# Score tiles of one or two PSUM banks: four narrow ones at a time in a fused transformer block

## The chip, the cores and the metric

The kernel runs on one core of a Trainium2 chip. The metric is the device time of one execution in microseconds (us); lower is better. TensorE is called PE below, its weight loads PEld, VectorE DVE, ScalarE ACT, GpSimd POOL, and SyncE, which issues the DMAs, SP.

## The reference

One block of a transformer on a sequence of 1024 positions, 1024 wide: a gated feed-forward network (2816 wide), a mixer, a second feed-forward network, with norms between. The mixer projects the input, runs two attentions and merges them through gates:

```python
# differential attention: 8 heads, two softmaxes each, causal, blocks of 128 queries
s = jnp.einsum('bqhcd,bkhcd->bhcqk', qb, k) * scale
p = softmax(where(kpos <= qpos, s, NEG_INF))
o = einsum('bhqk,bkhe->bqhe', p[:, :, 0] - lam * p[:, :, 1], v)
# sparse attention: 16 heads in 2 groups, three branches, weighted by gates
o = g[..., 0:1] * o_cmp + g[..., 1:2] * o_slc + g[..., 2:3] * o_win
y = x + (sigmoid(g_a) * (y_da @ w_proj_da) + sigmoid(g_b) * (y_ns @ w_proj_nsa)) @ w_out
```

At this length the selected branch (`o_slc`) takes in all earlier blocks, so it is a causal attention; the window branch (`o_win`) sees the last 512 positions. A block of 128 queries with number i (0 to 7) so needs scores against 128(i+1) keys, and in the window branch against at most 640.

## The kernel before, in words

The program is written as tiles from pools, and its waits and the order of instructions on each engine are set when it is built: a planner simulates the time line, and at each step gives an engine the ready instruction of the highest priority. Priority is the order of the program text, moved by offsets. On the chip each engine then follows that fixed order, and an instruction that isn't ready holds up all behind it on its engine.

Stages, in order: first feed-forward network (`ffn`), mixer (`mix`: `prelim`, `da_phase`, `ns_phase`), merging (`proj`), second feed-forward network. Products in fp32 precision are made of three matmuls of high and low parts (`mm3`, lines 52 to 54).

`da_phase` (differential attention) first runs the last projections of the stage before on the PSUM pool `gm0`, four tiles of 128x512 on the right side of PSUM, and closes it (`cg.close()`). Then it loops over 8 heads h and, in each, over m = 0..3, which is two blocks of queries (i = 2m and 2m+1). For each block and each of the two softmaxes, `scores` writes q·k into a score tile `S` in PSUM (L871, two matmuls, or four if the width is over 512), DVE adds the mask in place and finds the row maximum (L878), ACT writes the exponential into SBUF (`Pt`, L880) and so frees the tile. `da_pv` transposes the probabilities on PE into `tr` (L926), ACT and DVE split them (`th` L89, `tl` L85), and PE multiplies them with the values into `o` (L948 to 950). After the scores of each block, `fill.step` puts in a few matmuls of later projections (`gm`, the filler), ordered behind the last score matmul and at a lower priority; it uses PSUM pool `gm1`, one tile.

`ns_phase` (sparse attention) has the same form. Pairs of heads are taken for half H = 0 (m = 0, 1) and then H = 1 (m = 2, 3); each block has a score tile of the selected branch (`Ps`) and one of the window branch (`Pw`). Its matmuls with values are at L1083 and L1084, the compressed branch goes into `o` at L1049, and `ns_fold` (L1092, L1093) empties `o`.

Widths are 128(i+1), so blocks 0 to 3 (m = 0, 1; H = 0) have score tiles of up to 512 columns and blocks 4 to 7 (m = 2, 3; H = 1) of 640 to 1024, in two pieces. All score tiles come from one pool in each attention (`sp1`, `sp2`): two tiles of 1024 columns, which is two banks of 512 each, whatever the width. In each attention the open PSUM pools are, from the left: the scores (2 x 2 banks), `tr` (2), `o` (1), `gm` (1). In the stage ahead, `tr0` (2 banks) and `sc0` (2) lie on the left and `gm0` (4) on the right; in `proj`, `tot2` (2), then `pj` (4).

Every pool is opened with `reuse_waits="tile"`: where a pool lies on banks of a closed one, each of its tiles waits for the users of earlier tiles on its own banks alone.

Of the kernel before, what the change touches and what calls it, by code (L numbers as in the profile page):

```python
# [7 lines left out]
F32 = mybir.dt.float32  # L8
# [10 lines left out]
P = 128  # L19
T = 1024  # L20
TB = 512
# [22 lines left out]
def open_pool(K, ctx, name, bufs, psum=False, side=None):  # L44
    kw = {"space": PSUM} if psum else {}
    if side:
        kw["side"] = side
    return ctx.enter_context(K.tc.tile_pool(name=name, bufs=bufs, reuse_waits="tile", **kw))
# [29 lines left out]
def drain(units):  # L78
    for u in units:
        for _ in u:  # L80
            pass
# [780 lines left out]
        nc.sync.dma_start(out=K.s_pc[u * 2 + pr][tb], in_=pp.bitcast(F32))  # L862


def scores(K, passes, w, mask, nm, pt, l):
    nc = K.nc
    S = K.sp.tile([P, T], F32, tag="S", name="S")
    pieces = [(0, 0, w)] if w <= TB else [(0, 0, w // 2), (TB, w // 2, w // 2)]
    for o, c, n in pieces:
        for i, (q, k, k0) in enumerate(passes):  # L870
            K.last = nc.tensor.matmul(S[:, o:o + n], lhsT=q, rhs=k[:, k0 + c:k0 + c + n], start=i == 0, stop=i == 1)  # L871
    if w <= TB:
        sv, mv, pv = S[:, 0:w], mask, pt[:, 0:w]
    else:
        sv = S.rearrange("p (b c) -> p b c", b=2)[:, :, 0:w // 2]
        mv = mask.rearrange("p (b c) -> p b c", b=2)
        pv = pt[:, 0:w].rearrange("p (b c) -> p b c", b=2)
    nc.vector.tensor_tensor_reduce(out=sv, in0=sv, in1=mv, scale=-0.125, scalar=BIG, op0=ALU.add, op1=ALU.min,  # L878
                                   accum_out=nm)
    return nc.scalar.activation(out=pv, in_=sv, func=AF.Exp, scale=-1.0, bias=nm, accum_out=l)  # L880
# [81 lines left out]
def da_finish2(K, h, H, ob, sq):  # L962
    nc = K.nc
    tot = K.tr.tile([P, TB], F32, tag="tr", name="tot")
    nc.tensor.matmul(tot, lhsT=K.ones, rhs=sq, start=True, stop=True)
    m = K.op.tile([P, TB], F32, tag="sq", name="m")
    nc.vector.tensor_scalar(out=m, in0=tot, scalar1=1.0 / P, scalar2=EPS, op0=ALU.mult, op1=ALU.add)
    y = K.op.tile([P, TB], F32, tag="yr", name="yr")
    z = K.op.tile([P, TB], F32, tag="zr", name="zr")
    newton_rsqrt(nc, y, z, m, nc.gpsimd)  # L970
    nc.vector.scalar_tensor_tensor(out=ob, in0=ob, scalar=K.hgain[:, h:h + 1], in1=y, op0=ALU.mult, op1=ALU.mult)
    yo = [K.op.tile([P, TB], F32R, tag=t, name="yo") for t in ("yr", "zr")]
    split(nc, yo[0], yo[1], ob)
    for i in range(2):
        nc.sync.dma_start(out=K.s_yda[H][h][:, i], in_=yo[i].bitcast(F32))
# [329 lines left out]
def da_phase(K, cg):  # L1305
    nc = K.nc
    with ExitStack() as ctx:
        K.kp, K.vp, K.qp = open_pool(K, ctx, "dk", B_DK), open_pool(K, ctx, "dv", B_DV), open_pool(K, ctx, "dq", B_DQ)
        K.nk, K.vv = {}, {}
        for n, f in enumerate(da_units(K, 0)[:2] + da_units(K, 1)):  # L1310
            if n == 2:
                early = da_load_parts(K, 0)
            if n >= 2:
                next(early)
            if n == 5:
                q0 = da_queries(K, 0, 0)
            drain([f()])
        cg.close()
        K.low = LOW_DA
        log_exp(K)  # L1320
        K.pp, K.sm, K.tp, K.op = (open_pool(K, ctx, "dp", B_DP), open_pool(K, ctx, "dsm", 6), open_pool(K, ctx, "dt", B_DT),
                                  open_pool(K, ctx, "do", 1))
        K.sp = open_pool(K, ctx, "sp1", 2, True)
        K.tr = open_pool(K, ctx, "tr1", TR_DA, True)
        K.ops = open_pool(K, ctx, "o1", 1, True)
        K.gm = open_pool(K, ctx, "gm1", 3 - TR_DA, True)
        pend = K.fin = None

        def finish(h, m, res):
            if m % 2 == 0:  # L1330
                K.o = K.ops.tile([P, TB], F32, tag="o", name="o")
            if K.fin:
                da_finish2(K, *K.fin)
                K.fin = None
            da_pv(K, h, m, res, K.o)
            if m % 2 == 1:
                K.fin = da_finish(K, h, m // 2, K.o)

        ng = NG_DA // 2
        W = K.A["win"]  # L1340
        units = []
        for p in (2, 3):
            cs = [[C_QDA + 2 * p, C_QDA + 2 * p + 1], [C_KDA + 2 * p, C_KDA + 2 * p + 1], [C_VDA + 2 * p], [C_VDA + 2 * p + 1]]
            units += [(f, [W[c] for c in ws]) for f, ws in zip(da_units(K, p), cs)]
        units += [(f, [W[C_GATE + c]]) for c, f in enumerate(gate_units(K, range(16)))]
        units += [(lambda d=d: pda_unit(K, d), [K.A["wda"][d]]) for d in range(KD)]
        fill = K.filler = Filler(K, units)
        for p in range(4):
            fill.pace(4 * (p + 1) if p < 2 else 8 + ng * (p - 1), PACE_DA)
            for h in (2 * p, 2 * p + 1):  # L1350
                if h:
                    da_load(K, h)
                for m in range(4):
                    qt = q0 if h + m == 0 else da_queries(K, h, m)
                    if h == 4:
                        ns_load_key(K, m)
                    res = da_scores(K, h, m, qt, fill.step)
                    if pend:
                        finish(*pend)
                    pend = (h, m, res)  # L1360
            fill.end()
        finish(*pend)
        da_finish2(K, *K.fin)


def ns_phase(K):
    nc = K.nc
    K.low = LOW_NS
    with ExitStack() as ctx:
        K.wslab = open_pool(K, ctx, "wsl", 1).tile([P, 5 * P], F32, name="wslab")  # L1370
        nc.sync.dma_start(out=K.wslab, in_=K.A["wslab"])
        K.qp, K.kp, K.pcp = open_pool(K, ctx, "nq", 2), open_pool(K, ctx, "nk", 1), open_pool(K, ctx, "npc", B_NPC)
        K.pp, K.sm, K.tp, K.op = (open_pool(K, ctx, "np", B_NP), open_pool(K, ctx, "nsm", 6), open_pool(K, ctx, "nt", B_NT),
                                  open_pool(K, ctx, "no", B_NO))
        K.sp = open_pool(K, ctx, "sp2", 2, True)
        K.tr = open_pool(K, ctx, "tr2", 2, True)
        K.ops = open_pool(K, ctx, "o2", 1, True)
        K.gm = open_pool(K, ctx, "gm2", 1, True)
        fill = K.filler
        fill.pace(8 + 16 + KD, PACE_NS)  # L1380
        ns_load_values(K)
        pend = None

        def finish(hd, m, res, st, g, par):
            if m % 2 == 0:
                K.o = K.ops.tile([P, TB], F32, tag="o", name="o")
            ns_pv(K, hd, m, res, K.o, st[0], g, par)
            if m % 2 == 1:
                ns_fold(K, par, K.o, st[1])
                if par:  # L1390
                    ns_out(K, hd // 2, m // 2, st[1])

        for g in range(2):
            for pr in range(4 * g, 4 * g + 4):
                for H in range(2):
                    pc = K.pcp.tile([P, 2, TB], F32R, tag="pc", name="pc")
                    nc.sync.dma_start(out=pc.bitcast(F32), in_=K.s_pc[pr][H])
                    y = K.op.tile([P, TB], F32, tag="y", name="y")
                    for par in range(2):
                        hd = pr * 2 + par  # L1400
                        qt = []
                        for z in range(2):
                            t = K.qp.tile([P, TB], F32R, tag=f"q{z}", name="qt")
                            nc.sync.dma_start(out=t.bitcast(F32), in_=K.s_qns[hd // 4][z:z + 2, :, hd % 4, :, H * TB:(H + 1) * TB]
                                              .rearrange("h a d t -> (h a) d t"))
                            qt.append(t)
                        for m in (2 * H, 2 * H + 1):
                            res = ns_scores(K, hd, m, qt, g, fill.step)
                            if pend:
                                finish(*pend)  # L1410
                            pend = (hd, m, res, (pc, y), g, par)
        fill.end()
        if pend:
            finish(*pend)


def proj(K, open_x, after):
# [54 lines left out]
def body(tc, A, out):  # L1472
    nc = tc.nc
    K = Ctx()
    K.tc, K.nc, K.A = tc, nc, A
    K.low, K.vv, K.gate, K.fill, K.seen = 0, {}, None, None, {}
    K.h, K.acc, K.R = [None] * 2, [None] * 2, [None] * 2
    with ExitStack() as ctx:
        const = open_pool(K, ctx, "const", 1)
# [172 lines left out]
```

## Time and profile before

| | |
|---|---|
| time, median of 3 runs | 2951.38 us (2950.32 to 2952.54) |
| the profiled execution: time, span | 2957.75 us, 2955.7 us |
| PE busy | 2830.8 us, 96% of the span |
| DVE, ACT, POOL busy | 68%, 46%, 27% |
| granted TensorE clock, mean | 0.986 |

The two attentions lie at about 972 to 2109 us of the span. A row of the time line gives start, duration, engine, line, what it writes and reads, the operands' sizes, how many instructions are merged, and in brackets the idle time of the engine before it with what ended that. A row of waits gives the total, how often, and the longest.

### The profile page before, as it was taken

What the parts mean: (1) busy time and instruction counts of PE and PEld (TensorE: products, weight loads), DVE (VectorE), ACT (ScalarE), POOL (GpSimd) and SP (SyncE); (2) the same over time, 40 slices, a digit from 0 to 9 for tenths busy, and PEclk for the clock granted to TensorE, in tenths of its full rate; (3) what the DMA queues carried; (4) which work ended last, traced back from release to release, by engine and by line L of the source; (5) the groups of instructions that cost most, each with busy time, mean ns of one, the idle gap of its engine ahead of it and who ended that gap; (6) DMA issues with size and microseconds to landing.
All of it is one profiled execution on the core that took longest, in us unless ns stands there. A gap on an engine that the chain in (4) does not pass through costs nothing. (4 is left out here: it accounts for less than half of the span.)

```text
span 2955.7 us, 40158 instructions
## 1 busy us (share of the span) xinstructions
PE 2830.8 (96%) x14276; PEld 2129.2 (72%) x14276; DVE 2002.1 (68%) x3347; ACT 1366.1 (46%) x2347; POOL 788.7 (27%) x701
## 2 busy tenths in 40 slices
PE   8999999999999899989899999999999999999998
PEld 6644447888888678778788888888778854444886
DVE  7866856666687467667677777776343877675666
ACT  7543424442332245445466666666332653342443
POOL 3133321000144123322233323332242413333001
PEclk9999999999999999999999999999999999999999
DMA  4355548655456544444332234222742246454854
GB/s 161 129 194 180 182 161 287 214 172 170 146 200 240 173 161 168 170 165 164 122 115 79 86 119 155 79 84 76 281 158 100 89 147 230 149 185 158 297 182 146
DMA packets 212711, 478.20 MB, mean 162 GB/s; under 512 B 20896, under 2 KB 39584, under 8 KB 212512
## 3 DMA queue, kind: packets, MB, share of 16 engines
q1 hardware_dynamic: 212512, 475.65, 47.1%
q8 instruction: 112, 1.84, 0.3%
q14 instruction: 87, 0.71, 0.1%
HBM read 313.56 MB, written 162.00 MB: 161 GB/s over the span
## 5 line engine op out<-in xcount | busy, mean ns | idle before, releaser
L405 PEld LDWEIGHTS <-w 128*128 128x128 f16 x3024 | 297.1, 99 | 381.1 <-issue 30.4
L52 PE MATMUL gm<-hi,whi 128*128 128x512 f32 x880 | 351.5, 399 | 4.0 <-ACT whi L89 1.6
L54 PE MATMUL gm<-hi,wlo 128*128 128x512 f32 x880 | 348.3, 397 | 1.1 <-DVE wlo L85 1.1
L53 PE MATMUL gm<-lo,whi 128*128 128x512 f32 x880 | 348.0, 395 | 0.0
L405 PE MATMUL Y<-tf,w 128*128 128x512 f16 x1296 | 296.7, 383 | 19.1 <-DVE u L443 15.6
L871 PE MATMUL S<-kt,qt 128*128 128x320 f32 (+5 forms) x1152 | 274.6, 352 | 37.5 <-ACT Pt L880 12.0
L85 DVE TENSOR_TENSOR tl<-tr,th 128x512 fp32r<-128x512 f32 (+2 forms) x384 | 236.3, 619 | 89.0 <-ACT th L89 85.5
L89 ACT ACTIVATE th<-tr 128x512 fp32r<-128x512 f32 (+2 forms) x384 | 203.7, 542 | 200.4 <-PE tr L926 195.6
L85 DVE TENSOR_TENSOR wlo<-st,whi 128x1024 fp32r<-128x1024 f32 x154 | 197.6, 1300 | 113.5 <-ACT whi L89 112.2
L878 DVE CUSTOM_DVE_ANT_0 S<-S,slab 128x896 f32<-128x896 f32 (+7 forms) x320 | 224.7, 709 | 65.8 <-PE S L871 61.3
L53 PE MATMUL acc<-wlo,whi 128*128 128x512 f32 (+1 forms) x628 | 244.1, 389 | 1.0 <-DVE wlo L85 1.0
L89 ACT ACTIVATE whi<-st 128x1024 fp32r<-128x1024 f32 x154 | 160.7, 1057 | 178.2 <-PE acc L54 111.6
L54 PE MATMUL acc<-whi,wlo 128*128 128x512 f32 (+1 forms) x628 | 242.8, 389 | 0.0
L52 PE MATMUL acc<-whi 128*128 128x512 f32 (+1 forms) x628 | 240.4, 387 | 0.0
L871 PEld LDWEIGHTS S<-kt,qt 128*128 128x128 f32 x1152 | 183.4, 190 | 61.5 <-ACT Pt L880 13.8
L1037 POOL TENSOR_SCALAR Ps<-Ps,l 128x384 f32<-128x384 f32 (+7 forms) x128 | 100.7, 787 | 428.6 <-DVE l L1035 214.4
L405 PE MATMUL X<-h,w 128*128 128x512 f16 x864 | 195.3, 379 | 0.5 <-ACT s L415 0.5
L52 PEld LDWEIGHTS gm<-hi,whi 128*128 128x128 f32 x880 | 168.3, 191 | 37.2 <-ACT whi L89 2.2
L54 PEld LDWEIGHTS gm<-hi,wlo 128*128 128x128 f32 x880 | 167.8, 191 | 37.3 <-DVE wlo L85 1.8
L53 PEld LDWEIGHTS gm<-lo,whi 128*128 128x128 f32 x880 | 168.1, 191 | 30.9
L85 DVE TENSOR_TENSOR wlo<-wst,whi 128x1024 fp32r<-128x1024 f32 x103 | 135.8, 1320 | 45.4 <-ACT whi L89 36.1
L1083 PE MATMUL o<-th,vt 128*128 128x256 f32 (+1 forms) x608 | 165.0, 288 | 1.6 <-ACT th L89 1.5
(320 smaller groups left out, 6128.7 us busy)
## 6 DMA issues: line engine op xcount, KB each, us to landing
wst<-in_win_dram SPq DMA_DIRECT2D x55, 512.0 KB
sw<-w2s SPq DMA_DIRECT2D x44, 512.0 KB
st<-sw SPq DMA_DIRECT2D x88, 256.0 KB
st<-saT SPq DMA_DIRECT2D x88, 256.0 KB
a<-in_f1w_dram SPq DMA_DIRECT2D x36, 512.0 KB
a<-in_f2w_dram SPq DMA_DIRECT2D x36, 512.0 KB
st<-saB SPq DMA_DIRECT2D x66, 256.0 KB
qt<-sq SPq DMA_DIRECT2D x128, 128.0 KB
```

Source lines behind the costliest of these rows:

```text
L52: first = nc.tensor.matmul(out, lhsT=w[0][:, wk], rhs=x[0], start=start, stop=False, skip_group_check=skip)
L53: nc.tensor.matmul(out, lhsT=w[0][:, wk], rhs=x[1], start=False, stop=False, skip_group_check=skip)
L54: nc.tensor.matmul(out, lhsT=w[1][:, wk], rhs=x[0], start=False, stop=stop, skip_group_check=skip)
L85: return nc.vector.tensor_tensor(out=lo, in0=src, in1=hi.bitcast(F32), op=ALU.subtract)
L89: nc.scalar.activation(out=hi, in_=src, func=AF.Copy)
L405: K.mark = nc.tensor.matmul(o, lhsT=w[:, a, m * h + k], rhs=x[k][:, b], start=start and k == 0 and i == 0, stop=k == h - 1 and i == 2, ski ...
L871: K.last = nc.tensor.matmul(S[:, o:o + n], lhsT=q, rhs=k[:, k0 + c:k0 + c + n], start=i == 0, stop=i == 1)
L878: nc.vector.tensor_tensor_reduce(out=sv, in0=sv, in1=mv, scale=-0.125, scalar=BIG, op0=ALU.add, op1=ALU.min, accum_out=nm)
L1037: nc.gpsimd.tensor_scalar(out=p[:, 0:n], in0=p[:, 0:n], scalar1=l[:, c:c + 1], scalar2=1.0, op0=ALU.mult, op1=ALU.mult)
L1083: nc.tensor.matmul(dst, lhsT=v, rhs=hi[:, b * P:(b + n) * P], start=False, stop=False, skip_group_check=True)
```

## The change

`scores` takes its tile from a new function `score_tile`. Up to 512 columns the tile is one bank, from a pool of four such tiles; above, it is two banks, from a pool of two. The pool is opened when the first tile of a width class is asked for, and closed and opened anew where the class changes; it lies on the right side of PSUM. The fixed pools `sp1` and `sp2` go, and each attention ends with a `close_scores`.

```diff
+def score_tile(K, w):
+    n = 1 if w <= TB else 2
+    if K.s_banks != n:
+        close_scores(K)
+        K.sp, K.s_banks = open_pool(K, K.s_ctx, "sp", 4 // n, True, side="right"), n
+    return K.sp.tile([P, n * TB], F32, tag="S", name="S")
+
+
+def close_scores(K):
+    K.s_ctx.close()
+    K.s_ctx, K.s_banks = ExitStack(), 0
+
+
 def scores(K, passes, w, mask, nm, pt, l):
     nc = K.nc
-    S = K.sp.tile([P, T], F32, tag="S", name="S")
+    S = score_tile(K, w)
...
@@ da_phase
-        K.sp = open_pool(K, ctx, "sp1", 2, True)
         K.tr = open_pool(K, ctx, "tr1", TR_DA, True)
...
         da_finish2(K, *K.fin)
+        close_scores(K)
...
@@ ns_phase
-        K.sp = open_pool(K, ctx, "sp2", 2, True)
         K.tr = open_pool(K, ctx, "tr2", 2, True)
...
             finish(*pend)
+        close_scores(K)
...
@@ body
+    K.s_ctx, K.s_banks = ExitStack(), 0
```

The other pools of an attention so move to the left: `tr` to the first two banks, then `o`, then `gm`; the scores take the last four.

## The prediction

> **What bounds the kernel now.** I read the page first, then busy times by stage, then what PE waited for in each stage, then the time line around the longest waits.
>
> ```profile
> span 2955.7 us, 40158 instructions
> PE 2830.8 (96%) x14276; PEld 2129.2 (72%) x14276; DVE 2002.1 (68%) x3347; ACT 1366.1 (46%) x2347; POOL 788.7 (27%) x701
> L871 PE MATMUL S<-kt,qt 128*128 128x320 f32 (+5 forms) x1152 | 274.6, 352 | 37.5 <-ACT Pt L880 12.0
> ```
>
> PE is the bound: 125 us of its span are idle, and 37.5 of them lie ahead of score matmuls. The change moves no arithmetic off PE, so it can win only idle time. By stage (the columns are the stretch, its length, then busy time and count for PE, PEld, DVE, ACT, POOL, the granted clock, the DMA share, GB/s):
>
> ```profile
> 963.00:1040.00 77.00, 63.30 (x273) 51.32 (x273) 37.59 (x71) 20.73 (x38) 11.48 (x11) 0.91 0.50 172
> 1040.00:1455.00 415.00, 390.19 (x2061) 330.82 (x2060) 297.17 (x611) 207.13 (x425) 116.25 (x116) 0.98 0.47 162
> 1455.00:1480.00 25.00, 17.36 (x84) 14.23 (x85) 9.91 (x21) 9.50 (x21) 4.86 (x5) 0.80 0.34 115
> 1480.00:2090.00 610.00, 588.27 (x3752) 523.93 (x3751) 440.87 (x1134) 382.22 (x882) 187.82 (x259) 0.99 0.30 101
> ```
>
> These rows are the start of the differential attention, its body, the passage to the sparse attention, and that one's body. PE is idle 13.7, 24.8, 7.6 and 21.7 us in them. A score tile is freed by the exponential of L880, so a score matmul that waits for a free tile shows as a wait for ACT at L880. The waits of PE, first for the body of the differential attention, then for the sparse one:
>
> ```profile
> PE S L871 <- ACT Pt L880: 10.9, 7, 5.7
> PE o L948 <- ACT th L89: 3.9, 1, 3.9
> ...
> PE S L871 <- ACT Ps L880: 7.1, 14, 1.0
> PE o L1049 <- DVE y L1093: 5.2, 7, 1.1
> PE o L1084 <- DVE tl L85: 4.0, 15, 0.3
> PE S L871 <- ACT Pw L880: 3.3, 8, 0.9
> ```
>
> So waits for a score tile cost PE 10.9 us in the one and 10.4 us in the other. That 21.3 us, 0.7% of the time, is what more tiles could touch at most, and only the part in narrow blocks (up to 512 columns) is touched at all: a wide block has two tiles of two banks before and after.
>
> **The change part by part.** It adds and removes no instruction of the engines; it changes how many narrow tiles are open, which banks the pools have, and through both the order that the planner writes.
>
> *Sparse attention, narrow blocks.* One narrow stretch (H = 0 of a pair of heads) and the wide one behind it, then the time line of its start on PE and ACT:
>
> ```profile
> PE S L871 <- ACT Ps L880: 1.0, 2, 0.8
> PE o L1049 <- DVE y L1093: 0.6, 1, 0.6
> PE o L1084 <- DVE tl L85: 0.6, 2, 0.3
> PE S L871 <- ACT Pw L880: 0.4, 1, 0.4
> ...
> PE S L871 <- ACT Pw L880: 0.2, 1, 0.2
> ```
>
> ```profile
> 1538.96 0.44 PE L871 MATMUL S<-kt,qt 128*128 128x128 f32 x2 [0.22 <-ACT Ps L880]
> 1540.51 0.44 PE L871 MATMUL S<-kt,qt 128*128 128x128 f32 x2 [0.78 <-ACT Ps L880]
> 1544.80 0.39 PE L871 MATMUL S<-kt,qt 128*128 128x256 f32 x1 [0.39 <-ACT Pw L880]
> 1537.70 1.11 ACT L880 ACTIVATE Ps<-S,nm 128x1024 f32<-128x1024 f32 x1 [1.95 <-PE tr L926]
> 1539.99 0.37 ACT L880 ACTIVATE Ps<-S,nm 128x128 f32<-128x128 f32 x1 [0.22 <-DVE nm L878]
> ```
>
> The first narrow tile (1538.96) waited for the last 1024-wide exponential, which ends at 1538.81. After the change it needs a bank of that same wide tile, so its 0.22 us stay. The second (1540.51) waited for the first narrow one's exponential (1539.99 + 0.37); after, it takes the other bank of the wide tile and goes at once: 0.78 won. The third (1544.80) waited for the other wide tile; a bank of the first narrow tile has been free since 1540.36: 0.39 won. That is 1.17 of the 1.39 us. I found this pattern in five of the eight narrow stretches (from 1538, 1615, 1767, 1846 and 1997): 5.9 us. The first stretch (from 1478) has waits of its own, 1.04, 0.86 and 0.17 us, all between narrow tiles: 2.1 us. Together 8.0 us. What is late next is in the same rows: `o` waits for `ns_fold` (0.6) and for `tl` (0.6) in each stretch, and PE comes to them earlier by what it won. I let a quarter go there: −6 us, bounds −8 and −2.
>
> The Trainium skill, "TensorE: Matmul & The Clock Gate", section "HAM oscillation", reports a kernel in which PSUM double-buffering gave no further gain once the order of its loops kept PE fed. Here PE is 96% fed (588.27 of 610), so as a rule it speaks against this change: this term would be near 0 instead of −6, and the sum near no change. No row of before can show which it is; the rows above have PE idle before score tiles all the same, and the sum goes by them.
>
> *Differential attention, narrow blocks.* Of the 10.9 us three waits, 7.3 us, stand before narrow tiles; the matmul's size and count tell narrow from wide (two matmuls, not four):
>
> ```profile
> 1253.54 0.50 PE L871 MATMUL S<-kt,qt 128*128 128x256 f32 x2 [0.33 <-ACT Pt L880]
> 1270.58 1.22 PE L871 MATMUL S<-kt,qt 128*128 128x512 f32 x2 [5.67 <-ACT Pt L880]
> 1411.19 0.44 PE L871 MATMUL S<-kt,qt 128*128 128x128 f32 x2 [1.27 <-ACT Pt L880]
> 1269.37 0.60 ACT L89 ACTIVATE vh<-tr 128x512 fp32r<-128x512 f32 x1 [5.61 <-DMA sv<-vh]
> ```
>
> The long one is not for want of tiles in itself: ACT stood 5.61 us behind a filler's copy that waited for a store to land, and the exponential was queued behind it. With four tiles that score matmul would not have waited, and PE had `o` products and a filler behind it; but an ACT that stands stops the next thing too, and the new order needn't put the copy at that place. I take half: −3.7 us, bounds −7.3 and 0.
>
> *Start of the differential attention.* This is where the banks move. Before, the scores lie on the banks of `tr0` and `sc0`, long free, while the last projections still run on `gm0`. So the planner let the first scores run ahead among them:
>
> ```profile
> 963.00:1036.00 73.00, 7.03 (x32) 5.94 (x32) 0.91 0.51 173
> 972.05 0.45 PE L871 MATMUL S<-kt,qt 128*128 128x128 f32 x1 [4.31 <-issue]
> 977.83 0.66 PE L871 MATMUL S<-kt,qt 128*128 128x128 f32 x2 [4.26 <-DMA kt<-sk]
> 1011.48 0.66 PE L653 MATMUL tr<-ident,vt 128*128 128x128 f32 x4 [2.63 <-DVE vt L650]
> 1021.18 0.66 PE L653 MATMUL tr<-ident,vt 128*128 128x128 f32 x4 [1.05 <-DVE vt L650]
> 993.42 1.23 DVE L85 TENSOR_TENSOR rl<-m,rh 128x1024 fp32r<-128x1024 f32 x1 [12.25 <-DMA sq<-rl]
> ```
>
> The first row is the score matmuls alone: 7.0 us of PE up to 1036. After the change the scores lie on the right, on `gm0`'s own banks, and the first one has to wait until the last projections have emptied them, so these 7.0 us move behind. Against it, the two waits of 4.31 and 4.26 us, in which PE held the projections back for a score operand that had not landed, go. But the next bound there is already in the rows: DVE stood 12.25 us until 993.42 for a store to land, and the projections' results can't be evicted before that; with four banks PE would run about 21 us from 967 (24 matmuls at 0.23 us a tile, four tiles) and stop at 989. So I count the 8.6 us as turned into a wait for eviction, except some 2 us for an earlier restart. Of the 7.0 us, about 2.5 us were in the shadow of the waits at 1011 and 1021 and of the lower clock (0.91 in the first row), and return as idle or fall away. So −2 + 4.5 = +2.5 us. Ends: −8.6 (both waits go and nothing replaces them) and +11 (all 7.0 exposed, and 4 us of the first chain from score to transpose, of the size of the 4.3 us waits above, with no filler to cover it, since the filler is ordered behind the first score).
>
> *End.* `pj` of `proj` lay on banks of `S` and `tr`; after, its four are those of `o`, `gm` and two of `S`.
>
> ```profile
> 2109.30 0.44 PE L52 MATMUL pj<-yl,whi 128*128 128x512 f32 x1
> 2110.12 0.69 DVE L1093 TENSOR_TENSOR y<-o,y 64x512 f32<-64x512 f32 x1 [1.26 <-ACT y L1092]
> ```
>
> If the planner gives the first tile `o`'s bank, it waits for the fold, to 2110.81: 1.5 us. Three other banks are free, so I take +0.3, bounds 0 and +1.5. *Changes of width.* From narrow to wide, a wide tile needs two neighbouring banks, at worst with the last narrow tile in one; before, the second wide tile waited for it anyway. I count nothing, up to +3 over 16 changes of about 0.2 us, the size of the wide waits above. *DMA queue, POOL.* Nothing is moved past them; 0. *New order as such.* The planner's clock isn't the chip's; the 3.9 us wait for `th` shows what one misplacement costs, either way: 0, ±6.
>
> Sum: −6 − 3.7 + 2.5 + 0.3 = −6.9 us. The profiled execution took 2957.75 us (span 2955.7), 6.4 us over the median of 2951.38; the difference is applied to the median: 2944.5 us, −0.23%. Differences within 0.2%, 5.9 us, can't be told from no change here.
>
> **The rivals.**
> (a) *The stalls only change their names.* In the sparse attention the chain from transpose through `th` and `tl` to `o`, and the fold, take over what the tile waits leave; the differential one's long wait comes back elsewhere. For it: DVE is 72% and ACT 63% busy there (440.87 and 382.22 of 610). Against: waits at the fold and `tl` are short (0.3 to 1.1). With −2, 0 and the start's +2.5: 2952 us.
> (b) *Slower through the start.* Scores locked out by `gm0`: +11 there, with −2 and −2 kept of the two gains: 2958 us. It decides from about +10 at the start if the gains hold fully. For it: the row of 7.0 us run ahead. Against: PE's own stalls at 972 and 978 go.
> (c) *Pool by pool.* Reopening makes the first tile of a new width wait for all tiles of the old pool. A tile's chain at 512 columns is about 1.5 us (DVE 0.7, ACT 0.7 by their rows' rates), at some 30 changes, half covered: +22, with the sum 2966 us. Against: the pools are declared to wait tile by tile.
> (d) *The start gains too.* Both 4.3 us waits go without a successor, and the narrow waits go fully: −8 − 7.3 − 2 = 2934 us.
>
> **How the numbers follow.** Chances: forecast 0.40 (its own range 2938 to 2950), (a) 0.22, (b) 0.16, (c) 0.06, (d) 0.16. Faster by over 0.2%: (d) and three quarters of the forecast, 0.46. Same: a quarter of the forecast and (a), 0.32. Slower: (b) and (c), 0.22. The range takes in the forecast, (a), most of (d) and (b): 2932 to 2958.
>
> **What would show it.** Right: waits of narrow `S` for ACT at L880 in the sparse attention down from about 9 us to under 3; no score matmul before the last `gm0` projection; the gaps at 972 and 978 gone, with idle PE around 990 to 1000. Wrong: scores still among the projections; new long waits of PE for `th`, `tl` or the fold; waits at the first tile of each width. The whole would be wrong if the new order moved a DMA-bound wait into or out of the differential attention, which no row of before can tell.

## The result, and the profile after

The changed kernel is slower: 2996.24 us median (2994.45 to 2999.07) against 2951.96 us, a ratio of 1.0149 (95% interval 1.0132 to 1.0167). Its profiled execution took 2994.96 us, span 2992.9 us. From its page (columns as before):

```profile
span 2992.9 us, 40061 instructions
PE 2836.7 (95%) x14276; PEld 2130.5 (71%) x14276; DVE 2004.5 (67%) x3347; ACT 1367.3 (46%) x2347; POOL 794.0 (27%) x701
L884 PE MATMUL S<-kt,qt 128*128 128x320 f32 (+5 forms) x1152 | 260.3, 350 | 23.0 <-ACT Pw L893 6.9
```

The idle time ahead of score matmuls fell from 37.5 to 23.0 us, as intended, and yet PE's idle time rose from 125 to 156 us. (`scores` moved down by 13 lines: L884 was L871, the exponential L893 was L880.) The two attentions as two stages, from 963 to the first sparse score matmul and from there to the first `pj`; first before, then after:

```profile
963.00:1456.00 493.00, 453.53 (x2334) 382.22 (x2333) 335.45 (x683) 228.04 (x463) 128.59 (x128) 0.97 0.48 164
1456.00:2109.00 653.00, 622.51 (x3942) 552.11 (x3942) 458.17 (x1165) 398.68 (x914) 191.81 (x263) 0.99 0.32 108
```

```profile
963.00:1488.00 525.00, 462.70 (x2343) 387.84 (x2341) 336.71 (x681) 229.85 (x463) 134.71 (x129) 0.94 0.45 154
1488.00:2149.00 661.00, 624.28 (x3950) 552.11 (x3950) 461.95 (x1169) 400.12 (x916) 193.56 (x264) 0.99 0.32 108
```

The first stage takes 32 us longer: 22.8 us more idle PE (62.3 against 39.5) and 9.2 us more busy time, at a clock of 0.94 instead of 0.97. Not all of it is lost there. Up to the first score matmul PE has the same order of matmuls in both kernels, and yet this execution is already 3.6 us behind at 963; its first stage so holds 0.8% more matmul columns (909,184 against 902,144), some 3.5 us of the 9.2. The sparse attention takes 8 us longer, 6.2 of them idle.

The start, on PE's time line:

```profile
1005.61 0.80 PE L52 MATMUL gm<-hi,whi 128*128 128x512 f32 x1 [12.49 <-ACT whi L89]
...
1038.47 1.86 PE L884 MATMUL S<-kt,qt 128*128 128x128 f32 x7 [1.41 <-DVE vl L85]
```

The lockout is there: the first score matmul comes at 1038.47 instead of 972, and the two waits of 4.3 us have become one of 12.49 us. PE's waits in the body of the differential attention (1040 to 1456), then in the sparse attention (1520 to 2140):

```profile
PE gm L52 <- DVE vl L85: 12.6, 2, 12.1
PE o L961 <- DMA vt<-sv: 8.0, 3, 3.7
PE S L884 <- DMA qt<-sq: 6.6, 5, 3.9
PE o L962 <- DVE tl L85: 4.6, 4, 2.3
PE gm L52 <- DVE m L626: 4.0, 3, 2.1
PE S L884 <- ACT Pt L893: 2.6, 4, 1.0
```

```profile
PE o L1097 <- DVE tl L85: 11.4, 30, 2.4
PE o L1096 <- ACT th L89: 7.0, 9, 3.1
PE S L884 <- ACT Pw L893: 6.9, 22, 0.6
```

In the first, the wait for a score tile fell from 10.9 to 2.6 us, and five other names took its place. In the second, the waits for `Ps` and the fold are gone (7.1 and 5.2 us before), those for `Pw` rose from 3.3 to 6.9, and `o` waits 18.4 us for `tl` and `th`. The longest stall, followed through SP, ACT and DVE:

```profile
1267.32 0.69 DVE L85 TENSOR_TENSOR yo<-ob,yo 128x512 fp32r<-128x512 f32 x1
...
1275.47 4.76 SPq L988 DMA_DIRECT2D syd<-yo  x1
1281.00 1.09 SPq L988 DMA_DIRECT2D syd<-yo  x1
...
1287.54 0.63 ACT L155 ACTIVATE yr<-m 128x512 f32<-128x512 f32 x1 [10.44 <-DMA syd<-yo]
1290.19 0.60 ACT L89 ACTIVATE vh<-tr 128x512 fp32r<-128x512 f32 x1 [2.02 <-DMA sv<-vh]
1290.83 0.69 DVE L85 TENSOR_TENSOR vl<-tr,vh 128x512 fp32r<-128x512 f32 x1 [12.56 <-ACT vh L89]
...
1291.58 0.79 PE L52 MATMUL gm<-hi,whi 128*128 128x512 f32 x1 [12.08 <-DVE vl L85]
```

`yo`, a head's normalised result, is done at 1268.01; its store waits its turn on SP until 1275.47, and the second half until 1281.00. The next norm (`yr`) shares `yo`'s buffer, so ACT stands 10.4 us; the filler's copy `vh` is behind it on ACT, `vl` behind that on DVE, and PE's next filler needs the bank that `vl` empties. But `vh` then stands 2.02 us more for a store of its own buffer (`sv<-vh`), issued on SP at 1282.18, behind the second half of `yo`. So without the wait of `yr` this stall would have ended hardly earlier; what both waits share is SP's queue.

### The profile page after: what moved, and what is told of

The parts are those of the page before. It is cut to its first block, busy times and chain, and to the rows that moved or that the text cites. A ratio compares the mean times of both kernels' runs of the same rounds, so it can differ in the third digit from the quotient of the medians.

```text
span 2992.9 us, 40061 instructions
## 1 busy us (share of the span) xinstructions
PE 2836.7 (95%) x14276; PEld 2130.5 (71%) x14276; DVE 2004.5 (67%) x3347; ACT 1367.3 (46%) x2347; POOL 794.0 (27%) x701
## 5 line engine op out<-in xcount | busy, mean ns | idle before, releaser
L405 PE MATMUL Y<-tf,w 128*128 128x512 f16 x1296 | 297.1, 384 | 21.8 <-DVE u L443 18.4
L884 PE MATMUL S<-kt,qt 128*128 128x320 f32 (+5 forms) x1152 | 260.3, 350 | 23.0 <-ACT Pw L893 6.9
L884 PEld LDWEIGHTS S<-kt,qt 128*128 128x128 f32 x1152 | 184.2, 192 | 41.5 <-ACT Pw L893 12.2
L1097 PE MATMUL o<-tl,vt 128*128 128x256 f32 (+1 forms) x608 | 158.5, 293 | 13.0 <-DVE tl L85 12.5
```

The costliest lines, as they stand in the source:

```text
L405: K.mark = nc.tensor.matmul(o, lhsT=w[:, a, m * h + k], rhs=x[k][:, b], start=start and k == 0 and i == 0, stop=k == h - 1 and i == 2, ski ...
L1097: nc.tensor.matmul(dst, lhsT=v, rhs=lo[:, b * P:(b + n) * P], start=False, stop=last, skip_group_check=True)
```

## The experiments

**The three parts of the change.** T1: the banks (the lockout) are the loss. T2: the four tiles, through the order that the planner writes. T3: reopening. Also T0: any new order is a new throw.

Banks alone (two tiles of two banks, not reopened):

```diff
-        K.sp = open_pool(K, ctx, "sp1", 2, True)
+        K.sp = open_pool(K, ctx, "sp1", 2, True, side="right")
...
-        K.sp = open_pool(K, ctx, "sp2", 2, True)
+        K.sp = open_pool(K, ctx, "sp2", 2, True, side="right")
```

> Only the banks move: the two score tiles of two banks are opened on the right, so that they lie on gm0's banks, and tr, o and gm come first on the left; two tiles everywhere, nothing reopened. T1 (the lockout at the start, and what follows from the banks): the change's loss is here; no score matmul before the last gm0 projection, first score near 1038 us instead of 972, and the time 15 to 44 us over before (some 2967 to 2996). T2 (four narrow tiles let the planner write an order with more stalls): the start alone costs, about +10 to +15 at the head of DA4, and the time ends at +7 to +15, with the differential attention's later stalls (the 12.1 us at 1291 of after) absent. T0 (any new order re-rolls what the planner and the chip disagree on): anywhere from -5 to +30, with stalls at places that neither before nor after has.

The change without the banks (the scores on the left; `gm`, `o` and `tr` opened on the right, on the banks of before):

```diff
-        K.sp, K.s_banks = open_pool(K, K.s_ctx, "sp", 4 // n, True, side="right"), n
+        K.sp, K.s_banks = open_pool(K, K.s_ctx, "sp", 4 // n, True), n
...
```

> The change with its banks as before: narrow blocks have four tiles, wide ones two, the pool is reopened where the width changes, but the scores stay on the left (free when the first score comes) and tr, o and gm on the banks that they had before. T1: scores run ahead among the last projections again (about 7 us of score matmuls before 1036), and the time is -7 to 0 against before. T2: the start is as before, and still the time is 15 to 30 us over before, with long waits in the body of the differential attention and waits of o for th and tl in the sparse one (18 us together against about 5 in before). T0: between.

Reopening alone; against the kernel just described:

```diff
-        K.sp, K.s_banks = open_pool(K, K.s_ctx, "sp", 4 // n, True), n
-    return K.sp.tile([P, n * TB], F32, tag="S", name="S")
+        K.sp, K.s_banks = open_pool(K, K.s_ctx, "sp", 2, True), n
+    return K.sp.tile([P, T], F32, tag="S", name="S")
```

> Reopening alone: two tiles of two banks for every width, on the left, the pool closed and opened again where the width changes. T1 and T2: within 3 us of before. T3 (reopening is what costs, by waits at the first tile of a new width or by the order that it makes): 15 to 30 us over before, as much as with four narrow tiles.

Two tiles, reopened, on the right (the changed kernel with the edit just shown, the side kept):

> The changed kernel with two tiles of two banks in place of four of one: scores on the right (gm0's banks), reopened at each change of width. With two tiles on the right and no reopening the time was +18.5 us over before; with reopening and two tiles on the left it was -11.5; the change itself +44. If four tiles are what costs: +5 to +20 over before (2957 to 2972). If it is the lockout together with reopening: +35 to +45.

Four narrow tiles on the left in one attention only, the other as before:

```diff
+    if K.s_ctx is None:
+        return K.sp.tile([P, T], F32, tag="S", name="S")
...
```

> Four narrow tiles in the sparse attention alone, on the left with the pool reopened; the differential attention is before's. By the prediction: -6 us (waits of narrow scores for the exponential down from 9 us to under 3, nothing in their place). By T2: +6 us, as after's sparse attention lost 6.2 from its first score to the first pj: the waits for a score tile fall, and o's waits for th and tl rise from about 5 to about 18 us. By T1: as the prediction, -6 to 0.

> Four narrow tiles in the differential attention alone, on the left (no lockout), with the pool reopened; the sparse attention is before's. With four narrow tiles in both (scores on the left) the kernel took 35 us more than before: +28 at the head of the sparse attention and +8 at its start. T2 (four narrow tiles change the order, and the loss is in the differential attention) says +22 to +30, with ACT waiting 20 us or more in all for the store of the head's result before it may write the next norm (yr, zr), as in the run with four tiles in both. T1 (banks alone) says within 5 us of before.

Three narrow tiles in place of four:

```diff
-        K.sp, K.s_banks = open_pool(K, K.s_ctx, "sp", 4 // n, True), n
+        K.sp, K.s_banks = open_pool(K, K.s_ctx, "sp", 3 if n == 1 else 2, True), n
```

> Three narrow tiles of one bank in place of four, else as four on the left (2987) and two on the left, reopened (2941). Theory B: between them, nearer to four, as two exponentials more than two tiles allow are still one too many: ACT's wait for the buffers 15 to 40 us, the time 2955 to 2980. If each order is its own throw: anywhere from 2935 to 2990, with no tie to that wait.

Measured, with before; "first sparse" and "to pj" are the time of the first sparse score matmul and the length from there to the first `pj`, from PE's time line of each trace, and each ratio is against runs of the kernel before that were taken with it. One trace differs from another by some us even where nothing was changed: at 963, ahead of every edit's effect on PE's order, these traces lie 1.6 us ahead of before's to 4.7 us behind it.

| score tiles | side | reopened | first sparse | to pj | median | ratio (95%) |
|---|---|---|---|---|---|---|
| two (before) | left | no | 1456.0 | 653.4 | 2952 | 1 |
| two | right | no | 1474.0 | 653.8 | 2970.69 | 1.0065 (1.0050 to 1.0080) |
| two | left | yes | 1454.9 | 641.4 | 2940.78 | 0.9963 (0.9948 to 0.9977) |
| two | right | yes | 1470.2 | 643.1 | 2959.13 | 1.0015 (1.0003 to 1.0028) |
| three narrow | left | yes | 1477.9 | 658.8 | 2980.36 | 1.0108 (1.0091 to 1.0124) |
| four narrow | left | yes | 1482.7 | 660.7 | 2987.23 | 1.0124 (1.0107 to 1.0141) |
| four narrow (after) | right | yes | 1488.1 | 661.0 | 2996.24 | 1.0149 (1.0132 to 1.0167) |
| four, sparse only | left | there | 1454.6 | 657.3 | 2959.99 | 1.0030 (1.0020 to 1.0039) |
| four, differential only | left | there | 1486.2 | 654.5 | 2981.77 | 1.0100 (1.0085 to 1.0115) |

The rows fit together. Banks alone came out in T1's range (+18.5 us), four tiles on the left a little over T2's (+35, of 15 to 30). The four tiles cost 46 us on the left (2987.23 to 2940.78) and 37 on the right: T2 is the loss, and T1 alone is not, since with no lockout at all the four tiles still end 35 us over before. The banks cost 18 us with two tiles, 9 with four. T3 turned out the other way: reopening by itself gains 11.5 us on either side. It acts in the sparse attention (641.4 against 653.4 and 643.1 against 653.8); the first sparse score comes only 1.1 and 3.8 us earlier. In the sparse attention each kind of tiles has its own length, to a few microseconds: about 654 us with two tiles, 642 reopened, 657 to 661 with four (or three) narrow ones. Compared matmul by matmul, PE has the same order there on both sides with two tiles reopened, and nearly the same in the two kernels with two that are not. T0 alone would not repeat itself so well. The effects of the four tiles in the two attentions add up: 7.8 + 29.3 = 37.1 against 35.0. Three tiles cost nearly as much as four; 2980.36 is at the edge of the 2955 to 2980 that was forecast.

**Why four tiles cost in the sparse attention.** The stage with two tiles, reopened, then with four tiles in it only; PE's matmuls there have the same number of columns in both (1,117,184):

```profile
1454.90:2096.30 641.40, 617.47 (x3944) 546.99 (x3945) 454.12 (x1165) 399.78 (x914) 194.09 (x263) 0.99 0.32 111
```

```profile
1454.60:2111.90 657.30, 624.36 (x3944) 552.27 (x3945) 460.22 (x1166) 399.80 (x914) 193.81 (x263) 0.99 0.32 108
```

Four tiles have 9.0 us more idle PE (32.9 against 23.9) and 6.9 us more busy time. PE's waits with four, then with two (both 1500 to 2090), and on the time line what stands at the start with four:

```profile
PE o L1099 <- DVE tl L85: 8.0, 27, 0.7
PE S L886 <- ACT Pw L895: 6.9, 22, 0.6
PE o L1098 <- ACT th L89: 3.5, 7, 0.6
```

```profile
PE o L1097 <- DVE tl L85: 6.8, 25, 0.5
PE o L1096 <- ACT th L89: 3.4, 6, 0.7
PE S L884 <- ACT Pw L893: 2.2, 8, 0.4
```

```profile
1492.06 0.63 ACT L89 ACTIVATE yo<-ob 128x512 fp32r<-128x512 f32 x1 [4.18 <-DVE ob L986]
1493.12 0.38 PE L1098 MATMUL o<-th,vt 128*128 128x256 f32 x1 [3.12 <-ACT th L89]
...
1497.89 1.16 DVE L85 TENSOR_TENSOR tl<-tr,th 128x384 fp32r<-128x384 f32 x2 [3.81 <-DMA syd<-yo]
1498.50 0.58 PE L1099 MATMUL o<-tl,vt 128*128 128x256 f32 x1 [2.57 <-DVE tl L85]
```

Past the start `o` waits about as long as with two tiles (11.5 against 10.2 us); there it is the score matmuls that wait more, for `Pw`. The rest of the idle time is at the start. With four tiles the scores and the fillers go out nearly in one run from 1476 to 1490; next in PE's order is `o`, and it waits. Its `th` stands on ACT behind the last head's norm of the differential attention (4.18 us), its `tl` on DVE for that head's store (3.81 us). In the kernel before, that run lasts from 1479 to 1497, and `o` follows it without a wait. The longer busy time goes with a lower granted clock around these gaps: 0.86 against 0.93 from 1456 to 1500, 0.94 against 1.00 from 1500 to 1540.

**Why they cost in the differential attention: the buffers behind the score tiles.** An exponential reads a score tile and writes into one of seven buffers (`dp`, 4 KB a partition each), which is freed when DVE has combined the two softmaxes (`Pt`, L927) or PE has transposed the result (L939). ACT's waits for such a buffer from 1040 to 1456, in before (the same figures with two tiles reopened), in after, and with four tiles on the left:

```profile
ACT Pt L880 <- DVE Pt L914: 3.3, 2, 2.6
```

```profile
ACT Pt L893 <- DVE Pt L927: 36.7, 18, 4.3
```

```profile
ACT Pt L893 <- DVE Pt L927: 41.2, 20, 3.1
...
ACT Pt L893 <- PE tr L939: 11.0, 4, 5.1
```

This separates all the kernels with seven buffers: 0.7 to 3.3 us with two tiles, 36 us or more with three or four. ACT works in order, so while it stands for a buffer, the copies behind it (`th`, `vh`, the norms) stand too. That the wait goes with the loss doesn't show yet that it makes it, so I changed the number of buffers both ways. Six, with two tiles:

```diff
-B_DP = 7
+B_DP = 6
```

> Two tiles of two banks, reopened, on the left, with six buffers for the exponentials' results in place of seven. Theory B: the same signature as with four tiles comes back, ACT waiting 20 us or more for DVE's Pt and PE's tr, and +10 to +40 us against 2941. Rival (the buffers don't bind): within 6 us of 2941.

```profile
ACT Pt L893 <- DVE Pt L927: 10.9, 7, 2.7
...
ACT Pt L893 <- PE tr L939: 8.4, 5, 5.0
```

The time was 2966.25 us (1.0050, 1.0035 to 1.0065), 25 us over the same kernel with seven, and the first sparse score at 1472.7 instead of 1454.9: the wait came back with the loss. It isn't alone there: ACT's wait for the fillers' weights rose as well, from 5.5 to 22.1 us. Eight, at the price of a query buffer:

```diff
-B_DQ = 4
+B_DQ = 3
...
-B_DP = 7
+B_DP = 8
```

> Four narrow tiles on the left, with eight buffers for the exponentials' results (dp, seven so far) and three for the queries (dq, four so far; the room for the eighth). In the kernels with four narrow tiles ACT waits 36 to 55 us of the differential attention for such a buffer (for DVE's Pt and for PE's tr, which free it), in those with two 1 to 3 us. Theory B (the limit moved from the score tiles to these buffers, and ACT, in order, stands with the copies of everything else behind it): that wait falls below 20 us and the time comes 15 us or more below four tiles with seven buffers (2987), nearer to its two-tile control. Rival (the stores on SP's queue around 1240 to 1350, or the lost cover of o, set it): the wait may fall, the time stays within 8 us of 2987 by more than the control moves.

> The control: two tiles of two banks, reopened, on the left, with the same eight and three buffers. With two tiles ACT waits 3 us for such a buffer, so an eighth is worth nothing; three query buffers may cost. Theory B: 0 to +12 us against two tiles with seven buffers (2941), all of it by later queries.

This told nothing: 3013.83 us (1.0213, 1.0198 to 1.0228) with four tiles, 2978.12 (1.0094, 1.0079 to 1.0109) with two; both waited for queries, 46.0 and 37.5 us (differential attention, to 1480), where 12 us of loss at most was forecast for the second.

So I took the room from the mask instead, with a control of seven each. Of the mask only the right half is kept, so these kernels mask the first half of a wide block wrongly; every instruction keeps its size:

```diff
-        K.slab = cst.tile([P, T], F32, name="slab")
-        nc.sync.dma_start(out=K.slab, in_=A["slab"])
+        K.slab = cst.tile([P, TB], F32, name="slab")
+        nc.sync.dma_start(out=K.slab, in_=A["slab"][:, TB:T])
...
+def half_mask(K, w):
+    if w <= TB:
+        return K.slab[:, TB - w:TB]
+    return K.slab[:, TB - w // 2:TB].unsqueeze(1).broadcast_to([P, 2, w // 2])
...
```

> Four narrow tiles on the left with eight buffers for the exponentials' results and all four query buffers; the room comes from the mask, of which only the right half is kept, so that wide blocks read that half twice (their mask is wrong in the first half, every instruction keeps its size). Theory B (the buffers of the results are the limit that the two extra tiles run into): ACT's wait for a buffer in the differential attention (54 us with four tiles and seven buffers) falls to under 35 and the time lies 10 to 30 us below the control with seven buffers and the same mask. Rival C (the planner's order with more tiles ahead meets the stores and the lost cover whatever the buffers): within 8 us of that control.

> The control for four tiles: the half mask alone, seven result buffers. All theories: within 5 us of four tiles on the left with the whole mask (2987), as no size of an instruction and no order changes.

> Two tiles of two banks, reopened, on the left, with eight result buffers, four query buffers and the half mask. Theory B: two tiles hardly wait for a buffer (3 us), so within 6 us of the control with seven (some 2941). If an eighth gains 10 us or more here, the buffers bind in both and don't explain the difference.

> The control for two tiles, reopened: the half mask alone, seven result buffers. All theories: within 5 us of the same with the whole mask (2941).

ACT's waits with four tiles and eight buffers, then with seven (1040 to 1456):

```profile
ACT Pt L899 <- DVE Pt L933: 27.1, 13, 3.6
...
ACT yr L155 <- DMA syd<-yo: 22.5, 4, 7.1
...
ACT Pt L899 <- PE tr L945: 3.6, 3, 2.0
...
ACT zr L157 <- DMA syd<-yo: 2.5, 1, 2.5
```

```profile
ACT Pt L899 <- DVE Pt L933: 41.0, 20, 3.1
...
ACT zr L157 <- DMA syd<-yo: 20.6, 3, 12.3
ACT yr L155 <- DMA syd<-yo: 18.8, 4, 11.2
...
ACT Pt L899 <- PE tr L945: 10.8, 4, 5.1
```

Four tiles: 2982.51 us with eight (1.0104, 1.0087 to 1.0121), 2992.11 with seven (1.0131, 1.0114 to 1.0148). Two tiles: 2942.48 (0.9966, 0.9955 to 0.9978) and 2946.06 (0.9979, 0.9970 to 0.9988). The controls lie 4.9 and 5.3 us over the same kernels with the whole mask, though PE's matmuls come in the same order. The wait for buffers fell from 51.8 to 30.7 us (both names), and the eighth buffer is worth 9.6 us to four tiles and 3.6 to two; the theory had asked for 10 at least. Nor is it clean: with four tiles the eighth buffer also changed PE's order in the differential attention, and PE's waits there (1040 to 1480) mostly changed their names: those for a score tile fell from 18.9 to 2.3 us, those for `th` rose from 8.2 to 11.2, for queries from 0.6 to 10.4, for `vl` to 9.2. It is a part, not the whole.

**The norm that waits for a store.** In the rows above ACT also waits 25.0 us (eight buffers) and 39.4 us (seven) for the head's store before it may write `yr` or `zr`. With four tiles on the left PE's longest wait of the differential attention, for a score tile, stands behind one of these, the exponential being next on ACT:

```profile
PE S L884 <- ACT Pt L893: 17.8, 6, 10.0
```

```profile
1342.12 0.63 ACT L157 ACTIVATE zr<-yr 128x512 f32<-128x512 f32 x1 [12.37 <-DMA syd<-yo]
...
1343.25 1.22 PE L884 MATMUL S<-kt,qt 128*128 128x512 f32 x2 [9.96 <-ACT Pt L893]
```

So there the wait for a score tile rose with four tiles, from 10.9 to 17.8 us (first row, 1040 to 1456). I took the store's wait away: the store reads a tile that stays (in the first two kernels the mask, in the last two a cosine table), so that `yo` is free at once and what is stored is not the heads' result.

```diff
-        nc.sync.dma_start(out=K.s_yda[H][h][:, i], in_=yo[i].bitcast(F32))
+        nc.sync.dma_start(out=K.s_yda[H][h][:, i], in_=K.slab[:, 0:TB])
```

> The changed kernel, but the 32 stores of the differential attention's normalised heads take the mask as their source instead of yo: the same DMAs of the same size at the same place, and no buffer of yo is held until its store lands (the values stored are not the heads'). In after, ACT waited 16 us in all (10.4 us the longest) for that store before it could write yr, and PE lost 12.1 us at 1291 behind it. If that wait is the loss of the differential attention's body: that stall is gone and the time is 12 to 22 us below after (2974 to 2984). If the stall is only the name of a new order that is short of DMA: another wait of 6 to 12 us stands in its place and the time is within 6 us of after.

> The same edit in the kernel before, as the control: in before ACT waited for that store 8.9 us in two places before 1500, none of which stopped PE for long. Expected: 0 to -5 us against before. If it gains as much as in the changed kernel (12 us or more), the store's wait is a loss of both kernels and does not explain their difference.

The changed kernel gained 14 us (2981.90; 1.0094, 1.0078 to 1.0111), the kernel before 7.6 (2944.91; 0.9978, 0.9969 to 0.9988), where 5 at most was forecast; so this wait explains some 7 us of their difference. And the stall at 1291 stayed, under another name:

```profile
1289.24 0.60 ACT L89 ACTIVATE vh<-tr 128x512 fp32r<-128x512 f32 x1 [10.03 <-DMA sv<-vh]
```

PE's filler at 1292.13 waited 11.02 us behind it. The store ahead of it on SP is now not ACT's problem; the filler's own store, on the same queue, is. Last, the eighth buffer and the free store together:

> Four narrow tiles on the left, eight result buffers, half mask, and the 32 stores of the normalised heads take their data from a table that stays (the values stored are not the heads'), so that no norm waits for a store. With eight buffers alone four tiles took 2982.5, ACT still waiting 25 us for those stores and 34 us for result buffers. If buffers and stores together are the loss of four tiles: 15 us or more below 2982.5, and within 20 us of its two-tile control. If the new order as such is (waits that only change names): within 10 us of 2982.5, and 30 us or more over the control.

> The control with two tiles, reopened: eight result buffers, half mask, the same stores from the table. With two tiles ACT hardly waited for stores or buffers (under 1 us each), so -8 to +2 us against the same kernel with yo stored (2942.5).

2972.16 us (1.0067, 1.0044 to 1.0089) with four tiles, 2940.44 (0.9958, 0.9945 to 0.9972) with two. This pair is the cleanest: from the first score matmul to the first `pj`, PE's matmuls come in the same order as without the free store, with four tiles and with two, and the gain is 10.3 us with four, 2.0 with two. The distance between four and two tiles went from 46.1 to 40.0 with the eighth buffer and to 31.7 us with the free store. Neither forecast of these runs held fully: 10.3 us came, not 15, and what is left is over 30 us.

So of some 46 us by which four narrow tiles are slower than two, the free store took 8.3 at an unchanged order of PE, and the eighth buffer 6.0 together with a new one. It took away less than half of the wait for buffers, so what the buffers hold in all isn't known. The sparse attention holds 15 to 19 us (660.7 against 641.4; with eight buffers 657.4 against 642.6); the rows show where PE waits there, but no run took one of those waits away. The rest, 13 to 17 us, is not settled. The order that the planner writes with more tiles open remains a rival for all but the store's part, as no run here has four tiles and two at the same order. Why reopening makes a better order in the sparse attention isn't settled either.

The fastest version that leaves nothing out is two tiles of two banks, on the left, reopened at each change of width: 2940.78 us, 0.37% below before (ratio 0.9963, 0.9948 to 0.9977) and 55 us below the change.

## Why the prediction was wrong, point by point

- *Sparse attention, −6.* Measured +7.6 (661.0 against 653.4), outside its bounds. Already its first half failed in part. The waits of narrow scores were to fall from about 9 us to under 3; counted tile by tile they fell from 9.3 to 5.8, as those for `Ps` went from 6.4 to 1.0 and those for `Pw` rose from 2.9 to 4.8. The other step that failed is "a quarter go there": over the whole stage `o`'s waits for `tl` and `th` rose from 10.2 to 20.8 us, more than was won, the fold's 5.2 included. That is rival (a)'s mechanism, which had put −2 on it, and 5.5 us of the rise are two waits near the start, behind the attention before. The rule weighed there (the Trainium skill, "TensorE: Matmul & The Clock Gate", "HAM oscillation": no further gain from double-buffering in PSUM, in its kernel) came nearer than the rows that I trusted, but it too gives no loss.
- *Differential attention, −3.7 (−7.3 to 0).* This is the step that cost the prediction: four tiles alone moved the first sparse score by +26.7 us (1482.7 against 1456.0). The step that failed is that a tile wait which goes is time won ("I take half"). In the changed kernel tile waits did fall, from 10.9 to 2.6 us, and yet PE's idle time up to the first sparse score rose from 39.5 to 62.3 us; with the same four tiles on the left, tile waits even rose, to 17.8, and idle time to 55.2. "An ACT that stands stops the next thing too" is what happened, at 1343 on the left. The prediction counted only PE's waits for a score tile. It did not ask where the exponentials of four tiles would put their results, with seven buffers held by the block before: ACT's waits for one, by both names, went from 3.3 to 41.6 us (52.2 on the left). And it did not count ACT's waits for stores. A free store and an eighth buffer took back 14 of the 46 us, over both attentions; the rest of the cause is open.
- *Start, +2.5 (−8.6 to +11).* Within its bounds. At equal work done (the sum of the matmuls' columns), the three kernels with scores on the right lie 3.4 to 5.3 us more behind before at 1040 than at 960. But those with scores on the left spread from 3.8 us less to 4.5 us more, so the size of this term is known only roughly. The turned wait was expected at 990 to 1000; it ended at 1005.61. The row of 4.31 us names `issue`, so that a score operand held PE there is not shown; the one of 4.26 us names it. What the banks cost beyond that came later, in the body: with two tiles on the right, not reopened, 18 us at the first sparse score.
- *End, +0.3 (0 to +1.5).* At the upper bound, for the reason given:

```profile
2149.09 0.50 PE L52 MATMUL pj<-yl,whi 128*128 128x512 f32 x1 [1.41 <-DVE y L1106]
```

- *Changes of width, 0 (to +3).* Reopening alone gave no loss, and rival (c) falls with it. It gained 11.5 us, which nothing in the prediction allowed.
- *New order as such, 0 ± 6.* Mis-sized, and with it the range. Kernels that differ only in banks, reopening or number of tiles lie from 11 us under to 44 over before; the banks alone are 18, the reopening alone 11.

Rival (b) named the right side, for a cause (the start) that holds some 4 of the 44 us; all that the banks cost beside four tiles is 9.

## What to carry to other kernels

Before a stage gets more tiles, follow one tile to where its result goes: if the next stage's buffers are already full when the tiles are, the wait moves there, onto an in-order engine, and can take what is queued behind it along. Waits of the bounding engine for a resource say roughly what that resource can give; they say nothing of what a planner does with more of it. Where an order is planned anew, the uncertainty of the order has to be measured with a neutral edit (here: reopen, or swap the sides) rather than guessed; and an edit that keeps the order (here the free store) says more than one that changes it (here the eighth buffer).

The Trainium skill, "Perfetto Trace Analysis", section "Optimization Strategy", says that the same gap repeating on the engine that should be saturated can mean too few buffers in SBUF or PSUM. Here the gaps for PSUM tiles were real (21.3 us of PE before), but with more tiles a shortage in SBUF came up, seen not on PE but in ACT's waits for result buffers (3.3 us before, 36.7 after); an eighth buffer, with the new order that it brought, gave 9.6 us.

## What the runs showed of the hardware

Instructions that issue a DMA are themselves held up on SP at times: mostly they take 0.3 to 0.6 us, but the store at 1275.47 took 4.76 us (row above), and the two queries ahead of it 4.25 and 4.85 us, while the DMA engines were busy for 0.26 of the time against 0.68 just before (first rows below). What holds them isn't shown, and the change didn't bring it: in the kernel before, the store of `yo` at 1271.5 took 4.09 us, and in both kernels 24 such instructions took over 2 us. A long stall costs PE more than its length. In the one that ended at 1291.58 the granted clock was 0.54 (1280 to 1291.5); it was 0.83 for the next 8.4 us, which I estimate from this row at 1.4 us lost (0.17 of 8.4), and 1.00 from 1300 to 1310. In the sparse attention, where two kernels had the same number of matmul columns, 9.0 us more idle time came with 6.9 us more busy time.

```profile
1240.00:1260.00 20.00, 16.32 (x76) 13.60 (x76) 15.33 (x28) 12.29 (x22) 5.03 (x6) 0.91 0.68 228
1260.00:1280.00 20.00, 17.24 (x92) 13.58 (x90) 13.99 (x34) 6.05 (x16) 4.51 (x5) 1.00 0.26 101
```

```profile
1280.00:1291.50 11.50, 0.00 (x0) 0.00 (x0) 0.67 (x1) 1.94 (x4) 0.00 (x0) 0.54 0.57 199
1291.60:1300.00 8.40, 8.40 (x38) 7.11 (x39) 5.93 (x11) 3.73 (x10) 5.04 (x5) 0.83 0.45 162
```
